# A retention stage run whole, and run as 16 pieces between other products, in a two-block network on one core

## The chip, the cores and the metric

The kernel runs on one core of one Trainium2 chip. The metric is the device time of one execution in microseconds (us), and lower is better. Five engines work beside each other: TensorE (PE, with its weight loads shown as PEld), VectorE (DVE), ScalarE (ACT), GpSimd (POOL) and SyncE (SP), which issues the kernel's DMAs from one queue in order. Each engine takes its instructions in the order in which the program puts them on it, and waits on semaphores for the others.

## The reference, cut to what matters

The network has two blocks of two layers each. The change touches the second block alone, and in it one part of each layer: from the normed input `h` (1024 tokens, 1024 features) one product gives the inputs of three branches, whose results are joined by `w_out`.

```python
za, xb, q, k, v, g = jnp.split(proj, splits, axis=-1)
ya = spatial_gating(jax.nn.gelu(za), a_vnorm_g[l], a_ws[l], a_bs[l])   # gated mixing over tokens
yb = multiscale_pool(xb, b_w[l], b_scale[l])                            # pooling
yc = retention(q, k, v, g, c_norm_g[l])                                 # retention
```

Retention has 8 heads of 64 features. In the reference it goes by chunks of tokens, in order, with a state per head that is carried on:

```python
scores = jnp.einsum('bnthd,bnshd->bnhts', qc, kc) * d_intra
y_intra = jnp.einsum('bnhts,bnshe->bnthe', scores, vc)
kv = jnp.einsum('bnshd,bnshe->nbhde', kc * k_dec[:, :, None], vc)
def step(state, kv_n):
    return state * chunk_dec[None, :, None, None] + kv_n, state
y_cross = jnp.einsum('bnthd,nbhde->bnthe', qc * q_dec[:, :, None], s_prev)
```

Mean and variance per head are then taken out, and the result is multiplied by `silu(g)`.

## The kernel before, in words

Large products (called dense here) keep float32 accuracy with two parts to each operand, `hi` and `lo`, and three matrix products per block (`mm3`, L221 to L223), each with 128 rows, 128 weight columns and 512 moving columns. A dense result of 128 x 512 takes 8 blocks, so 24 matmul instructions, and collects in one PSUM bank. `gemm_tm` makes results with tokens on partitions, the first two tokens' tiles as a pair; `gemm_fm` makes results with features on partitions. Weights come by DMA (`wraw`, three buffers) and are split by `load_w`: ACT casts `whi` (L205), DVE or, one time in six, POOL subtracts `wlo` (L192, L190). Four pairs of buffers hold weights (`wt`). After each dense result both call `tick`, which takes one step of a generator in `self.side`, if there is one; the first block uses this for its convolution.

`layer2` (per layer, twice) runs in this order:

1. `rotate`: queries and keys, rotated on DVE and written to DRAM by head (`rq_d`, `rk_d`).
2. `gemm_tm("v", ...)`: 8 tiles of values, each copied by ACT into `V` (L1073).
3. `retention`: 8 tiles of 128 tokens, one after the other.
4. `pooling_in`: four dense results, the inputs `xb` of the pooling.
5. `spatial_in`: 8 dense results `za` (L1094), the inputs of the gated mixing.
6. `pooling`: POOL adds shifted copies (L1157 to L1161), DVE finishes (L1164 to L1166).
7. `retention_out`: the retention result is scaled on DVE (L1296, L1297), the gate's 8 dense results follow, with `pooling_out` and `spatial` between them.

In one tile of `retention` TensorE has these small float32 products, each of which the trace shows as two instructions, except the transposes:

- scores, L1238: 8 products `sc<-rq,rk` of 64 rows, 128 columns. Even heads lie on partitions 0 to 63 (g = 0), odd heads on 64 to 127 (g = 1); first all four of one half, then all four of the other. DVE multiplies by the decay mask into `ra` (L1240).
- transposes of the keys, L1245: 4, `sc<-ident,rk`, which DVE scales into `kd` (L1247). Not for the last tile.
- intra-tile outputs, L1252: 8 products `ax<-rv,ra` of 128 rows, 64 columns, into `pi`.
- cross outputs, L1260: 8 products `sc<-rst,rq` of 64 rows with the state `rst`, again half by half; DVE scales (L1261) and adds (L1262). Not for the first tile.
- the tile's share of the state, L1270: 8 products `ax<-rv,kd` into `pv`; POOL and DVE make the next state (L1276, L1277). Not for the last tile.

Then the means: DVE reduces (L1280), POOL scales and subtracts into `V` (L1281, L1283), ACT squares (L1285), DVE reduces (L1286), and POOL raises to the power -0.5 (L179).

PSUM has three pools: `mm` (3 banks, dense results), `ax` (2 banks, `pi` and `pv` among others) and `sc` (3 banks, scores, transposes, cross outputs). A scheduler orders the instructions of each engine by the order of the code and by when buffers come free; in the built program it puts a few dense products of stage 4 between the tiles of retention.

```python
            self.gemm_tm("v", I["w_tm_v"][l], 512, toks(), ev_v)
            with left(f"re{l}", 2) as rp, left(f"re1{l}", 1) as r1:
                self.retention(l, V, rp, r1)
```

## Time and profile before

| | us |
|---|---|
| three timed runs, median | 3703.01 |
| lowest and highest of them | 3697.34, 3711.04 |
| span of the profiled execution | 3717.3 |
| TensorE busy in it | 3510.1 (94%) |
| VectorE, ScalarE, GpSimd busy | 2445.2, 1242.8, 849.8 |

The profiled execution is another one than the three timed runs; of its own time only the span is given, from its first instruction to its last, and what lies around it is not in the table. Its stages can be found by their lines. In the first layer of the second block the retention's first TensorE instruction starts 1565.3 us into the span and its last ends at 1627.4; in the second layer they are at 2684.2 and 2785.65.

### The profile page before, as it was taken

What the parts mean: (1) busy time and instruction counts of PE and PEld (TensorE: products, weight loads), DVE (VectorE), ACT (ScalarE), POOL (GpSimd) and SP (SyncE); (2) the same over time, 40 slices, a digit from 0 to 9 for tenths busy, and PEclk for the clock granted to TensorE, in tenths of its full rate; (3) what the DMA queues carried; (4) which work ended last, traced back from release to release, by engine and by line L of the source; (5) the groups of instructions that cost most, each with busy time, mean ns of one, the idle gap of its engine ahead of it and who ended that gap; (6) DMA issues with size and microseconds to landing.
All of it is one profiled execution on the core that took longest, in us unless ns stands there. A gap on an engine that the chain in (4) does not pass through costs nothing.

```text
span 3717.3 us, 46878 instructions
## 1 busy us (share of the span) xinstructions
PE 3510.1 (94%) x17414; PEld 2809.0 (76%) x17414; DVE 2445.2 (66%) x3786; ACT 1242.8 (33%) x2249; POOL 849.8 (23%) x700
## 2 busy tenths in 40 slices
PE   7979889999897999999999998999999989999998
PEld 4868656677875678887878777887897778888787
DVE  5965368568553866364599998437244479999645
ACT  4114146341241752113343333223102333443322
POOL 4332232112313222040132321001022032322100
PEclk9999989999997999999999999999959999999999
DMA  6222155542213243314322223424311622221532
GB/s 197 75 75 69 55 167 172 181 125 75 77 61 102 75 129 134 102 36 143 120 83 80 81 77 109 140 85 153 94 32 60 188 72 82 80 80 63 176 99 92
DMA packets 242965, 380.69 MB, mean 102 GB/s; under 512 B 24048, under 2 KB 99760, under 8 KB 242224
## 3 DMA queue, kind: packets, MB, share of 16 engines
q1 hardware_dynamic: 242736, 377.69, 31.9%
q8 instruction: 137, 2.24, 0.3%
q14 instruction: 92, 0.75, 0.1%
HBM read 280.35 MB, written 97.26 MB: 102 GB/s over the span
## 4 chain that ended last, share of the span: by engine, by line
PE 66%; DVE 14%; DMA 8%; issue 5%; ACT 2%; POOL 2%; SPq 1%; DVEq 0%; POOLq 0%; ACTq 0%
PE mm L221 11%; PE mm L222 11%; PE mm L223 11%; PE ax L221 3%; PE ax L223 3%; PE ax L222 3%; PE sc L221 3%; PE sc L222 3%; PE sc L223 3%; DVE wlo L192 2%; PE mm L943 2%; DVE ca L494 2%; PE mm L929 2%; DMA wraw<-ks_d 2%; DVE cv L1431 1%
## 5 line engine op out<-in xcount | busy, mean ns | idle before, releaser
L221 PE MATMUL mm<-hi,whi 128*128 128x512 f32 (+1 forms) x1780 | 693.7, 390 | 21.5 <-ACT whi L205 9.9
L223 PE MATMUL mm<-hi,wlo 128*128 128x512 f32 (+1 forms) x1780 | 690.3, 388 | 4.8 <-DVE wlo L192 3.7
L222 PE MATMUL mm<-lo,whi 128*128 128x512 f32 (+1 forms) x1780 | 691.4, 388 | 1.2 <-DVE lo L1616 1.1
L205 ACT CAST whi<-wraw 128x512 fp32r<-128x512 f32 (+3 forms) x412 | 232.1, 583 | 539.3 <-PE mm L222 258.7
L221 PEld LDWEIGHTS mm<-hi,whi 128*128 128x128 f32 x1780 | 339.0, 190 | 96.2 <-ACT whi L205 10.3
L223 PEld LDWEIGHTS mm<-hi,wlo 128*128 128x128 f32 x1780 | 338.6, 190 | 76.9 <-DVE wlo L192 6.0
L222 PEld LDWEIGHTS mm<-lo,whi 128*128 128x128 f32 x1780 | 339.2, 191 | 72.2 <-DVE lo L1616 3.1
L192 DVE TENSOR_TENSOR wlo<-wraw,whi 128x512 fp32r<-128x512 f32 (+2 forms) x320 | 228.7, 727 | 245.8 <-ACT whi L205 244.8
L221 PE MATMUL sc<-hi,whi 128*128 128x512 f32 x732 | 290.2, 397 | 13.1 <-ACT y L1496 7.5
L190 POOL TENSOR_TENSOR wlo<-wraw,whi 128x512 fp32r<-128x512 f32 (+3 forms) x92 | 132.7, 1449 | 723.6 <-ACT whi L205 645.3
L222 PE MATMUL sc<-lo,whi 128*128 128x512 f32 x732 | 290.1, 396 | 2.1 <-DVE lo L1616 2.1
L223 PE MATMUL sc<-hi,wlo 128*128 128x512 f32 x732 | 290.1, 396 | 1.2 <-DVE wlo L192 1.1
L221 PE MATMUL mm<-whi,hi 128*128 128x512 f32 (+2 forms) x704 | 260.7, 370 | 30.7 <-DVE ggt L341 16.4
L222 PE MATMUL mm<-wlo,hi 128*128 128x512 f32 (+2 forms) x704 | 256.9, 365 | 3.4 <-POOL wlo L190 2.3
L223 PE MATMUL mm<-whi,lo 128*128 128x512 f32 (+2 forms) x704 | 257.2, 365 | 0.0
L494 DVE SCALAR_TENSOR_TENSOR ca<-u,wh,ca 128x1024 f32<-128x1024 f32 (+1 forms) x180 | 197.6, 1142 | 0.6
L223 PE MATMUL ax<-hi,wlo 128*128 128x512 f32 x456 | 180.2, 395 | 2.4 <-DVE wlo L192 2.4
L221 PE MATMUL ax<-hi,whi 128*128 128x512 f32 x456 | 179.9, 395 | 1.9 <-DVE xn L1347 1.4
L222 PE MATMUL ax<-lo,whi 128*128 128x512 f32 x456 | 179.6, 394 | 0.0
L192 DVE TENSOR_TENSOR wlo<-wr,whi 128x512 fp32r<-128x512 f32 x200 | 175.8, 890 | 0.0
L221 PEld LDWEIGHTS sc<-hi,whi 128*128 128x128 f32 x732 | 139.4, 190 | 45.8 <-ACT y L1496 7.9
L221 PEld LDWEIGHTS mm<-whi,hi 128*128 128x128 f32 x704 | 135.0, 192 | 50.8 <-issue 19.1
(378 smaller groups left out, 6864.3 us busy)
## 6 DMA issues: line engine op xcount, KB each, us to landing
wr<-in_w_up SPq DMA_DIRECT2D x80, 512.0 KB
wraw<-in_w_fm SPq DMA_DIRECT2D x108, 256.0 KB
wm<-in_w_mod SPq DMA_DIRECT2D x96, 256.0 KB
wraw<-in_w_down SPq DMA_DIRECT2D x96, 256.0 KB
hid_d<-fth SPq DMA_DIRECT2D x44, 512.0 KB
wraw<-hid_d SPq DMA_DIRECT2D x88, 256.0 KB
wraw<-in_w_out SPq DMA_DIRECT2D x80, 256.0 KB
yl<-y_d SPq DMA_DIRECT2D x64, 256.0 KB
```

The source lines that it names most:

```text
L190: nc.gpsimd.tensor_sub(out, x, f(hi))
L192: nc.vector.tensor_sub(out, x, f(hi))
L205: nc.scalar.copy(hi[:, c], r)
L221: nc.tensor.matmul(ps, sh, mh, start=start, stop=False)
L222: nc.tensor.matmul(ps, sh, ml, start=False, stop=False)
L223: nc.tensor.matmul(ps, sl, mh, start=False, stop=stop)
L494: nc.vector.scalar_tensor_tensor(a, u[:, j:j + n], wh[:, c, j:j + 1], a, op0=ALU.mult, op1=ALU.add)
L929: nc.tensor.transpose(pt[:, j * 128:j * 128 + 128], P[:, h, kt * 128:kt * 128 + 128], self.ident)
L943: nc.tensor.matmul(po[half[u], :256], vst[:, vt, 64 * v:64 * v + 64], PT[kt][:, u * 256:u * 256 + 256], start=kt == 0, stop=kt == nkt - 1)
L1431: nc.vector.scalar_tensor_tensor(t[:, o:], x[:, 0:S - o], wc(2 - o), t[:, o:], op0=ALU.mult, op1=ALU.add)
```

## The change

`retention` becomes a generator with two `yield`s per tile, so 16 steps. It starts before the values' products and is stepped by `tick`. `RT = 2` lets the first two ticks pass; then one step follows each dense result of `gemm_tm("v")`, of `pooling_in` and of `spatial_in`. The first step of a tile (a-piece) holds the scores, the transposes and the loads of the next tile's queries and keys; the second (b-piece) holds the cross outputs, the state's products and the intra-tile outputs, in this order. In scores and cross outputs the two halves of the rows now take turns, each into its own PSUM bank, with TensorE's order fixed by `in_order`. `pooling` moves ahead of `spatial_in`. The rest of the diff takes comments out, so line numbers after the change are 1 to 21 higher.

```diff
+RT = 2
...
-            self.gemm_tm("v", I["w_tm_v"][l], 512, toks(), ev_v)
             with left(f"re{l}", 2) as rp, left(f"re1{l}", 1) as r1:
-                self.retention(l, V, rp, r1)
+
+                self.ticks = [None] * RT
+                self.side = self.retention(l, V, rp, r1)
+                self.gemm_tm("v", I["w_tm_v"][l], 512, toks(), ev_v)
                 with self.right(f"mp{l}") as mp, self.right(f"sg{l}") as sp:
                     xb = self.pooling_in(l, W, lat, mp)
+                    self.pooling(l, xb, mp)
                     z = self.spatial_in(l, toks, sp)
-                    self.pooling(l, xb, mp)
+                    run(self.side)
+                    self.side = None
...
+        halves = [(g, slice(64 * g, 64 * g + 64)) for g in range(2)]
+        nxt = load(0)
+        for j in range(8):
+            q, k = nxt
+
+            ps = [self.psC.tile([128, 512], F32, name="sc", tag="sc") for g in range(2)]
+            with self.in_order():
+                for m in range(4):
+                    for g, r in halves:
+                        nc.tensor.matmul(ps[g][:, m * 128:m * 128 + 128], k[r, m, :], q[r, m, :], start=True, stop=True)
...
+                nxt = load(j + 1)
+            yield
...
             if j:
+                pc = [self.psC.tile([128, 4, 64], F32, name="sc", tag="sc") for g in range(2)]
+                with self.in_order():
+                    for m in range(4):
+                        for g, r in halves:
+                            nc.tensor.matmul(pc[g][:, m, :], q[r, m, :], st[r, m, :], start=True, stop=True)
...
+            pi = self.psB.tile([128, 512], F32, name="ax", tag="ax")
+            for h in range(8):
+                hv = slice(h * 64, h * 64 + 64)
+                nc.tensor.matmul(pi[:, hv], A[h % 2][:, h // 2, :], V[:, j, hv], start=True, stop=True)
...
             self.rsqrt(ss[:, j, :], ss[:, j, :], 1.0 / 64)
+            yield
```

TensorE, first layer, with buffer numbers, which tell apart the PSUM banks of the two halves. Before, the end of one tile and the start of the next: the scores of one half, then those of the other.

```order
L1260 MATMUL sc_14394<-rst_14341,rq_14353 128x64 x4
L1270 MATMUL ax_14401<-rv_13303,kd_14376 64x64 x8
L1238 MATMUL sc_14426<-rq_14422,rk_14423 128x128 x4
L1238 MATMUL sc_14433<-rq_14422,rk_14423 128x128 x4
L1245 MATMUL sc_14440<-ident_78,rk_14423 128x128 x4
L221 MATMUL mm_14697<-hi_13154,whi_14687 128x512
```

After, the start of an a-piece: the last dense product of a pooling input, then scores that go to the two banks in turn (the pattern goes on for eight products).

```order
L223 MATMUL mm_14390<-lo_13179,whi_14380 128x512
L224 MATMUL mm_14390<-hi_13178,wlo_14381 128x512
L1250 MATMUL sc_14416<-rq_14295,rk_14296 128x128
L1250 MATMUL sc_14417<-rq_14295,rk_14296 128x128
L1250 MATMUL sc_14416<-rq_14295,rk_14296 128x128
```

TensorE took four products of one half before it turned to the other; now each product's neighbour is of the other half, and a whole dense result stands before the piece.

TensorE, first layer, without numbers. Before, one tile of retention, with the four dense products (L221 to L223) that the scheduler put into it:

```order
L1270 MATMUL ax<-rv,kd 64x64 x8
L1238 MATMUL sc<-rq,rk 128x128 x8
L1245 MATMUL sc<-ident,rk 128x128 x4
L223 MATMUL mm<-hi,wlo 128x512
L221 MATMUL mm<-hi,whi 128x512
L222 MATMUL mm<-lo,whi 128x512
L223 MATMUL mm<-hi,wlo 128x512
L1252 MATMUL ax<-rv,ra 128x64
L1260 MATMUL sc<-rst,rq 128x64 x4
L1252 MATMUL ax<-rv,ra 128x64 x7
```

After, the one place where two pieces of a tile (the sixth) stand close to each other, because the pair at the start of `spatial_in` ticks twice:

```order
L1250 MATMUL sc<-rq,rk 128x128 x8
L1259 MATMUL sc<-ident,rk 128x128 x4
L222 MATMUL mm<-whi,hi 128x512
L1271 MATMUL sc<-rst,rq 128x64
L223 MATMUL mm<-wlo,hi 128x512
L224 MATMUL mm<-whi,lo 128x512
L222 MATMUL mm<-whi,hi 128x512
L1271 MATMUL sc<-rst,rq 128x64 x7
L1280 MATMUL ax<-rv,kd 64x64 x8
L1284 MATMUL ax<-rv,ra 128x64 x8
```

Here four dense products stand between the pieces as before; at the other places 24 do.

POOL, first layer. Before, the last tiles' means, then the pooling's large adds (L1157 to L1161) in a row:

```order
L1281 TENSOR_SCALAR rmu<-rmu 128x8
L1283 TENSOR_TENSOR rv<-ry,rmu 128x512
L179 TENSOR_TENSOR rss<-rss,mhalf 128x8
L1157 TENSOR_TENSOR s_15081<-xb_14685 128x1024
L190 TENSOR_TENSOR wlo<-wraw,whi 128x512
L1158 TENSOR_TENSOR s_15082<-s_15081 128x1024
```

After, the same adds (L1162 to L1166) with the state's and the means' steps of two tiles behind and between them:

```order
L1162 TENSOR_TENSOR s_14658<-xb_14378 128x1024
L191 TENSOR_TENSOR wlo<-wraw,whi 128x512
L1163 TENSOR_TENSOR s_14659<-s_14658 128x1024
L1291 TENSOR_TENSOR rst<-rst,rgam 128x256
L1301 TENSOR_SCALAR rmu<-rmu 128x8
L1159 MEMSET s_14670 128x16
L1303 TENSOR_TENSOR rv<-ry,rmu 128x512
L1159 MEMSET s_14671 128x16
L180 TENSOR_TENSOR rss<-rss,mhalf 128x8
L1162 TENSOR_TENSOR s_14670<-xb_14517 128x1024
```

The pooling moved from behind the retention into its tiles 3 to 5. On every engine the rest of the program keeps its order; the counts of instructions are the same.

## Rows read from the trace of the kernel before

**Rows 1.** The page: span, TensorE's busy time, its granted clock in 40 slices.

```profile
span 3717.3 us, 46878 instructions
...
PEclk9999989999997999999999999999959999999999
```

**Rows 2.** Windows: length, busy time by engine, granted clock, DMA share, GB/s; by stage.

```profile
1565.30:1627.40 62.10, 61.93 (x533) 56.79 (x532) 39.75 (x77) 8.66 (x15) 23.58 (x27) 0.89 0.26 78
1627.40:1701.50 74.10, 73.02 (x315) 58.79 (x315) 35.03 (x48) 20.13 (x43) 24.27 (x15) 1.00 0.14 43
...
2684.20:2785.65 101.45, 99.93 (x533) 91.61 (x533) 42.13 (x80) 9.33 (x16) 26.05 (x28) 0.53 0.16 48
```

**Rows 3.** Windows again, at the falls of the granted clock.

```profile
1580.65:1584.35 3.70, 3.70 (x31) 3.56 (x30) 1.60 (x4) 0.63 (x1) 1.83 (x2) 1.00 0.27 75
1584.35:1591.17 6.82, 6.82 (x43) 6.02 (x42) 5.21 (x9) 0.63 (x1) 1.91 (x4) 0.50 0.16 48
...
1594.59:1601.41 6.82, 6.82 (x44) 6.26 (x44) 4.45 (x8) 0.63 (x1) 2.05 (x4) 0.50 0.13 38
...
2684.17:2690.27 6.10, 4.58 (x38) 4.03 (x38) 3.62 (x6) 2.15 (x5) 1.40 (x1) 1.00 0.46 139
2690.27:2789.25 98.98, 98.98 (x506) 90.44 (x506) 41.83 (x81) 7.17 (x12) 25.92 (x29) 0.50 0.14 41
```

**Rows 4.** Timeline of TensorE, one tile at full clock: start, length, line, tiles, count.

```profile
1602.19 1.10 PE L1260 MATMUL sc<-rst,rq 64*128 64x64 f32 x8
1603.22 1.77 PE L1252 MATMUL ax<-rv,ra 128*128 128x64 f32 x14
1604.93 1.10 PE L1260 MATMUL sc<-rst,rq 64*128 64x64 f32 x8
1605.96 0.69 PE L1270 MATMUL ax<-rv,kd 128*64 128x64 f32 x16
1606.58 1.71 PE L1238 MATMUL sc<-rq,rk 64*128 64x128 f32 x16
1608.22 0.66 PE L1245 MATMUL sc<-ident,rk 128*128 128x128 f32 x4
1608.63 0.48 PE L222 MATMUL mm<-lo,whi 128*128 128x512 f32 x1
1608.94 0.39 PE L223 MATMUL mm<-hi,wlo 128*128 128x512 f32 x1
```

**Rows 5.** Timeline of TensorE, the scores at half clock, second layer.

```profile
2732.15 3.09 PE L1238 MATMUL sc<-rq,rk 64*128 64x128 f32 x16
```

**Rows 6.** Timeline of TensorE where L1238 and L1260 take turns by chance.

```profile
1623.21 0.27 PE L1238 MATMUL sc<-rq,rk 64*128 64x128 f32 x1
1623.26 0.27 PE L1260 MATMUL sc<-rst,rq 64*128 64x64 f32 x1
1623.32 0.27 PE L1238 MATMUL sc<-rq,rk 64*128 64x128 f32 x1
```

**Rows 7.** Timeline of ACT: copies of two values' tiles, one dense result apart.

```profile
1537.38 0.59 ACT L1073 COPY rv<-mm 128x512 f32<-128x512 f32 x1 [5.01 <-PE mm L223]
1542.98 0.59 ACT L1073 COPY rv<-mm 128x512 f32<-128x512 f32 x1 [5.01 <-PE mm L223]
```

**Rows 8.** Timeline of DVE, POOL and ACT in one tile; in brackets idle time and its releaser.

```profile
1607.94 0.68 DVE L1280 TENSOR_REDUCE rmu<-ry 128x8 f32<-128x512 f32 x1
...
1608.54 1.28 DVE L1240 TENSOR_TENSOR ra<-sc,dm 128x512 f32<-128x512 f32 x2
...
1609.73 0.68 DVE L1247 TENSOR_TENSOR kd<-sc,rdec 128x512 f32<-128x512 f32 x1
...
1610.82 0.69 DVE L1286 TENSOR_REDUCE rss<-rsq 128x8 f32<-128x512 f32 x1 [0.41 <-ACT rsq L1285]
```

**Rows 9.** Timeline during the pooling's POOL adds: two DVE subtractions, TensorE's wait.

```profile
1650.26 5.16 DVE L192 TENSOR_TENSOR wlo<-wraw,whi 128x512 fp32r<-128x512 f32 x2
...
1655.48 0.50 PE L222 MATMUL mm<-wlo,hi 128*128 128x512 f32 x1 [1.08 <-DVE wlo L192]
```

More of the change, by code (lines that the diff above doesn't have):

```diff
@@ L1225, in retention, with load @@
         st = None
-        for j in range(8):
+        def load(j):
             tk = slice(j * 128, j * 128 + 128)
@@ L1232, in retention @@
                     out=t, in_=d[:, :, :, tk].rearrange("(m h) a f t -> (h a f) m t", h=2))
+            return q, k
+        halves = [(g, slice(64 * g, 64 * g + 64)) for g in range(2)]
[7 more added lines that the diff above has]
+                        nc.tensor.matmul(ps[g][:, m * 128:m * 128 + 128], k[r, m, :], q[r, m, :], start=True, stop=True)
             A = []
             for g in range(2):
-                ps = self.psC.tile([128, 512], F32, name="sc", tag="sc")
-                r = slice(64 * g, 64 * g + 64)
-                for m in range(4):
-                    nc.tensor.matmul(ps[:, m * 128:m * 128 + 128], k[r, m, :], q[r, m, :], start=True, stop=True)
                 a = rp.tile([128, 4, 128], F32, name="ra", bufs=3)
-                nc.vector.tensor_mul(a, ps.rearrange("p (h t) -> p h t", h=4), dm[:, g::2, :])
+                nc.vector.tensor_mul(a, ps[g].rearrange("p (h t) -> p h t", h=4), dm[:, g::2, :])
                 A.append(a)
@@ L1248, in retention @@
                                         dec[:, 0, :].unsqueeze(2).broadcast_to([128, 8, 64]), op=ALU.mult)
-            pi = self.psB.tile([128, 512], F32, name="ax", tag="ax")
-            for h in range(8):
-                hv = slice(h * 64, h * 64 + 64)
-                nc.tensor.matmul(pi[:, hv], A[h % 2][:, h // 2, :], V[:, j, hv], start=True, stop=True)
+                nxt = load(j + 1)
+            yield
             y = rp.tile([128, 8, 64], F32, name="ry", tag="ry", bufs=3)
-            piv = pi.rearrange("p (h d) -> p h d", h=8)
             if j:
-                for g in range(2):
-                    pc = self.psC.tile([128, 4, 64], F32, name="sc", tag="sc")
-                    r = slice(64 * g, 64 * g + 64)
-                    for m in range(4):
-                        nc.tensor.matmul(pc[:, m, :], q[r, m, :], st[r, m, :], start=True, stop=True)
-                    nc.vector.tensor_tensor(y[:, g::2, :], pc, dec[:, 1, g::2].unsqueeze(2).broadcast_to([128, 4, 64]), op=ALU.mult)
-                nc.vector.tensor_add(y, y, piv)
-            else:
-                nc.scalar.copy(y, piv)
+                pc = [self.psC.tile([128, 4, 64], F32, name="sc", tag="sc") for g in range(2)]
[3 more added lines that the diff above has]
+                            nc.tensor.matmul(pc[g][:, m, :], q[r, m, :], st[r, m, :], start=True, stop=True)
+                for g in range(2):
+                    nc.vector.tensor_tensor(y[:, g::2, :], pc[g], dec[:, 1, g::2].unsqueeze(2).broadcast_to([128, 4, 64]),
+                                            op=ALU.mult)
             if j < 7:
@@ L1270, in retention @@
                     nc.tensor.matmul(pv[r, (h // 2) * 64:(h // 2) * 64 + 64], kd[:, h, :], V[:, j, hv], start=True, stop=True)
+            pi = self.psB.tile([128, 512], F32, name="ax", tag="ax")
+            for h in range(8):
+                hv = slice(h * 64, h * 64 + 64)
+                nc.tensor.matmul(pi[:, hv], A[h % 2][:, h // 2, :], V[:, j, hv], start=True, stop=True)
+            if j < 7:
                 ns = rp.tile([128, 4, 64], F32, name="rst")
@@ L1278, in retention @@
                 st = ns
+            piv = pi.rearrange("p (h d) -> p h d", h=8)
+            if j:
+                nc.vector.tensor_add(y, y, piv)
+            else:
+                nc.scalar.copy(y, piv)
             mu = rp.tile([128, 8], F32, name="rmu")
```

## The prediction

> **What bounds the kernel now.** I read the page first. TensorE is busy in 94% of a span of 3717.3 us, so a time can only fall where TensorE has less to do or does it faster. The page's line of the granted clock has a 5 in the 30th of 40 slices, which is 2695 to 2788 us, and 7 to 9 elsewhere [rows 1]: there TensorE runs at the lower of its two levels, 1.2 for 2.4 GHz. Next I took the windows of the retention in both layers [rows 2]. The same 533 instructions take 62.10 us at a mean clock of 0.89 in the first layer and 101.45 us at 0.53 in the second. TensorE is busy in 61.93 and 99.93 us of them; DVE has 40 to 42 us of work in each, POOL 24 to 26. So TensorE itself is the limit, and its small products and their clock are the price, not a chain of waits.
>
> Then the clock's falls [rows 3]. In the second layer it falls at 2690.27, behind a stretch in which TensorE waited 1.5 of 6.1 us, and stays down for 98.98 us, in all of which TensorE is busy. In the first layer it falls twice for 6.82 us; ahead of the first fall lie 3.7 us with only cross outputs (L1260) and intra-tile outputs (L1252), 31 instructions, without any wait. Busy time alone does not hold the clock up; these small products do not.
>
> Last, one tile at full clock, by the starts of its groups [rows 4]. The scores (L1238) take 1608.22 - 1606.58 = 1.64 us, 103 ns for each of 16; transposes 0.41; the state's products (L1270) 0.62; cross outputs 1.03 per half, 2.06; intra-tile outputs 1.71 for 14, 1.95 for 16. Together 6.68 us. Eight tiles, the first without cross outputs (4.62), the last without transposes and state's products (5.65), make 50.3 us. At half clock the 16 scores last 3.09 us for 1.71 [rows 5].
>
> **The change part by part.** A dense result takes 1542.98 - 1537.38 = 5.60 us, or 0.233 us for each of its 24 products [rows 7]. In program order 23 dense products lie among the retention's rows in the first layer and 24 in the second. Their time leaves 62.1 - 5.4 = 56.7 us and 101.45 - 5.6 = 95.9 us for the retention, 152.6 us in both. Dense work is neither added nor removed, so only these 152.6 us change.
>
> *The halves in turn.* The trace of before has one place where products of the two halves mix: L1238 of one tile's second half and L1260 of the next work's first half start alternately, and a pair takes 1623.32 - 1623.21 = 0.11 us [rows 6]. Apart, the two take 0.103 + 0.129 = 0.23 us [rows 4]. I take 0.11 for each pair of scores and of cross outputs: 8 pairs, 0.89 us, for 1.64 and 2.06. The bounds are half of what they take now (0.82) and no gain at all (1.64 and 2.06); the mixed rows are the same lines and the same sizes, so I stand by them. A full tile is then 0.89 + 0.41 + 0.89 + 1.95 + 0.62 = 4.76 us, the first 3.87, the last 3.73, and a layer 36.2 us.
>
> *The clock.* A b-piece is the longest small stretch, 0.89 + 0.62 + 1.95 = 3.5 us, and a dense result of 5.6 us stands on either side but at one place. The clock fell behind 3.7 us of L1260 and L1252 alone; in a b-piece L1252 has 1.95 us, and the faster products stand ahead of it. Over the first 19 us of the first layer's retention, with L1270, L1238 and four dense products in each tile, it stayed up. I take full clock throughout.
>
> Weighed against this: the Trainium skill (TensorE: Matmul & The Clock Gate, section HAM oscillation) says that the clock drops where the engine goes idle between bursts. By that rule nothing in the pieces could lower it. The rows differ, 98.98 us at 0.50 without idle time [rows 3], and the measurement decides.
>
> *Edges.* The first dense product behind small ones starts 0.31 us ahead of the next, for 0.233 [rows 4]: 0.08 us for each of 16 pieces, 1.3 us a layer. So 37.5 us a layer, 75.0 in both, and 152.6 - 75.0 = 77.6 us saved.
>
> *Waits in the pieces.* A b-piece needs `ra` and `kd` from DVE: 1.28 + 0.68 = 2.0 us behind the a-piece [rows 8], hidden by 5.6 us of dense work. What may stand ahead of them on DVE is the tile before: its step L1286 waits for POOL's and ACT's, and ends 1611.51 - 1607.94 = 3.6 us behind the start of L1280 [rows 8], then come two scalings of `V`. That is some 6 us behind a b-piece, and the next a-piece ends 5.6 + 1.3 us behind it: the cover is there, with 3 to 4 us to spare before the b-piece. In the sixth tile only four dense products (0.93 us) and the cross outputs lie between; there TensorE may wait up to 1 us. During the pooling's large POOL adds DVE slows down: two subtractions of 0.7 us each took 5.16, and TensorE waited 1.08 for them [rows 9]. These adds now fall into tiles 3 to 5 of the retention, and `rst`, `rmu` and the subtraction queue behind them on POOL; DVE waits for POOL in turn, and the next `ra` stands behind that wait. I allow 2 us a layer for all of this, 0 to 8 as bounds. The wait at the first tile of the second layer (1.5 us [rows 3]) goes, since 24 dense products now cover it; it is in the 95.9.
>
> *Queues.* SP's loads of queries and keys stand between weight loads, as before; those for the third to fifth tile now precede the last part of the pooling's weights and the first of `za`. They wait for pieces 20 to 30 us ahead of the weights' use, so I cost them at nothing; without that cover each late weight would cost a few us. The first weights of the pooling lose the retention as cover; their buffer comes free early in the last values' result, which leaves 4 us and a b-piece for two casts and two subtractions.
>
> **Sum.** 77.6 - 4 = 73.6 us off the span of 3717.3 gives 3643.7. That span is 14.3 us above the median of the timed runs, 3703.0, and the runs differ by 13.7 among themselves. Why is not shown; if it is the length of the half-clock stretch, the median run has less to gain. So I take 71 us off the median: **3632 us**.
>
> **The rivals.**
>
> 1. *The halves do not overlap.* Then scores stay at 1.64 and cross outputs at 2.06: 8 x 0.75 + 7 x 1.17 = 14.2 us a layer, 28 in both, 3660. For it: rows 6 are one place, where the products were of different kinds. Against it: same sizes, same halves.
> 2. *Each edge drains TensorE.* With 16 pieces there are 32 edges a layer between dense and small products; at the whole 0.39 us of a dense product for each, 12.5 us a layer, 25 in both, 3657. Against it: the dense product behind the transposes came 0.08 us late [rows 4]. The Trainium skill (TensorEngine Tiling (Array Packing), section Key Properties) says that a change of tiling mode drains the engine, which speaks for this rival. By it the split would pay at every edge.
> 3. *Waits take the gain.* If DVE were late at each of the 8 b-pieces of a layer by 4.5 us, 72 us would go, and the time would be 3704, no change. It needs DVE to fall some 8 us behind in each tile. Against it: DVE has 40 + 35 us of work [rows 2] in a stretch that will be about 121 us a layer.
> 4. *The clock falls in the pieces.* A fall in the first layer lasted 6.82 us [rows 3], in which half, 3.4, is lost. One at each of the 32 pieces of both layers costs 109 us: 3741, slower. From 21 falls on it eats the gain. For it: 99 us at half clock with four dense products in each tile did not bring the clock back [rows 3]. Against it: now 24 do stand there, for four.
>
> That the pieces are not where they should be is excluded by the program's order.
>
> **How the numbers follow.** Forecast 0.79, between 3618 and 3648; no overlap 0.07; drains 0.03; waits 0.04; clock 0.05; something else 0.02. The range goes from 3612, which is 77.6 us and the other runs' spread below the median, to 3662, behind the first two rivals and the bound of 16 us of waits in both layers. About 0.5%, 18.5 us, is what a measurement can tell from no change. Faster by more: the forecast, the first two rivals and part of the rest, 0.90. Within 0.5%: 0.04. Slower: 0.06.
>
> **What would show it.** The line of the clock should have no 5 in its middle, and windows over the spread retention should read 1.00 or close. Scores and cross outputs should have starts 50 to 60 ns apart. From the end of the third values' tile to the last piece there should be 15 dense results, 84 us, and 37.5 us of pieces. TensorE's waits inside the pieces should add up to under 5 us a layer, the longest at the sixth tile. The prediction is wrong if a DVE or POOL step ends long waits ahead of L1280 or L1284, or if the windows around the b-pieces show 0.50.

## The result and the profile after

The changed kernel takes 3657.66 us, median of four runs (3651.94 to 3664.98), the kernel before 3705.76 (3697.34 to 3711.04), 48 us less. The ratio is 0.9882, 95% interval 0.9834 to 0.993; ratios here are estimates from the fast runs of a set (within 1.5% of the fastest) and differ a little from the quotient of the medians (0.987 here). The direction is the predicted one; the size is not. The forecast was 3632, 71 us less, with a chance of 0.79 for 3618 to 3648; the measured time lies outside of that, and inside the wider range of 3612 to 3662. Between the two profiled executions the gain is larger, 3717.3 - 3655.3 = 62.0 us of span. The time is the span and 1.8 us around it (3657.07 for 3655.3), so the profiled execution of the changed kernel lies amid its runs, and that of the kernel before, 3719, above all four of its own. That gap of 14 us turns out to be about half of the miss of 26.

The page of the changed kernel answers [rows 1]: the 5 in the 30th slice of the clock's line is gone.

```profile
span 3655.3 us, 46869 instructions
...
PEclk9989989999898999999999999999999999999999
```

Windows answer [rows 2, 3] (length, busy time of PE, PEld, DVE, ACT and POOL, granted clock, DMA share, GB/s): from the first to the last piece in each layer, then two parts of the second layer.

```profile
1536.76:1663.56 126.80, 125.00 (x868) 102.45 (x869) 62.80 (x106) 25.53 (x50) 42.64 (x37) 1.00 0.17 51
2643.15:2775.31 132.16, 129.22 (x868) 106.25 (x869) 62.15 (x106) 23.79 (x48) 41.35 (x37) 0.96 0.16 49
2731.41:2736.40 4.99, 2.05 (x15) 1.26 (x13) 3.18 (x5) 0.08 (x1) 1.31 (x1) 1.00 0.18 53
2736.40:2746.64 10.24, 10.24 (x57) 9.04 (x53) 3.25 (x6) 0.63 (x1) 1.85 (x3) 0.50 0.09 27
```

Of the 868 TensorE instructions 508 are the retention's own; the other 360 are the 15 dense results that the forecast counted, 84.0 us at 5.60. So the retention now costs 126.8 - 84.0 = 42.8 us in the first layer and 48.2 in the second, 91.0 together, for 152.6 before. 61.6 us less: that is the difference of the spans but for 0.4 us. The forecast had 79.0, its 4 us of waits included.

TensorE's timeline for one tile answers [rows 4 to 6] (start, length, line, count; dense rows left out).

```profile
1552.23 1.16 PE L1250 MATMUL sc<-rq,rk 64*128 64x128 f32 x16
1553.32 0.66 PE L1259 MATMUL sc<-ident,rk 128*128 128x128 f32 x4
...
1559.51 1.11 PE L1271 MATMUL sc<-rst,rq 64*128 64x64 f32 x16
1560.55 0.69 PE L1280 MATMUL ax<-rv,kd 128*64 128x64 f32 x16
1561.16 2.00 PE L1284 MATMUL ax<-rv,ra 128*128 128x64 f32 x16
```

By the starts, the scores take 1.09 us for 1.64 before and the cross outputs 1.04 for 2.06. Two products in turn cost 0.13 to 0.14 us, where the forecast took 0.11.

Last, the sixth tile of the second layer, where only four dense products lie between the two pieces: the timeline of all engines, with idle time and its releaser in brackets.

```profile
2721.67 1.89 POOL L1165 TENSOR_TENSOR s<-s 128x1024 f32<-128x1024 f32 x1
...
2725.00 2.38 POOL L1166 TENSOR_TENSOR s<-s 128x1024 f32<-128x1024 f32 x1
2727.34 1.04 POOL L1303 TENSOR_TENSOR rv<-ry,rmu 128x512 f32<-128x512 f32 x1
...
2728.42 0.63 ACT L1305 ACTIVATE rsq<-rv 128x512 f32<-128x512 f32 x1 [11.84 <-POOL rv L1303]
...
2729.83 0.69 DVE L1306 TENSOR_REDUCE rss<-rsq 128x8 f32<-128x512 f32 x1
...
2731.08 1.65 POOL L180 TENSOR_TENSOR rss<-rss,mhalf 128x8 f32<-128x8 f32 x1 [2.69 <-DVE rss L175]
...
2732.76 0.69 DVE L1317 TENSOR_TENSOR rv<-rv,rss 128x512 f32<-128x512 f32 x1 [1.76 <-POOL rss L180]
...
2734.09 1.28 DVE L1254 TENSOR_TENSOR ra<-sc,dm 128x512 f32<-128x512 f32 x2
2734.83 0.43 PE L1271 MATMUL sc<-rst,rq 64*128 64x64 f32 x2 [2.94 <-DVE ra L1254]
```

It is read from the bottom. TensorE stands 2.94 us for `ra`. DVE is late with `ra` since the scaling of the tile before (L1317) stands ahead of it and waits 1.76 us for POOL's power (L180). That power is late since the tile's subtraction (L1303) had queued behind the pooling's adds (L1165, L1166). 1.6 us behind the wait's end the clock falls for the 10.24 us of the fourth window above.

In the first layer the same chain stands at the same place, and the wait is shorter; no fall follows it (1.00 in the first window above).

```profile
1627.77 0.43 PE L1271 MATMUL sc<-rst,rq 64*128 64x64 f32 x2 [1.64 <-DVE ra L1254]
```

### The profile page after: what moved, and what is told of

It reads as the page before. It is cut to its first block, busy times and chain, and to the rows that moved or that the text cites. A ratio compares the mean times of both kernels' runs of the same rounds, so it can differ in the third digit from the quotient of the medians.

```text
span 3655.3 us, 46869 instructions
## 1 busy us (share of the span) xinstructions
PE 3441.3 (94%) x17414; PEld 2743.3 (75%) x17414; DVE 2447.5 (67%) x3786; ACT 1239.3 (34%) x2249; POOL 850.9 (23%) x700
## 4 chain that ended last, share of the span: by engine, by line
PE 61%; DVE 14%; DMA 9%; issue 6%; ACT 3%; POOL 3%; SPq 1%; DVEq 0%; POOLq 0%; ACTq 0%
PE mm L222 11%; PE mm L223 11%; PE mm L224 11%; PE ax L223 3%; PE ax L224 3%; PE ax L222 3%; PE sc L223 3%; PE sc L222 3%; PE sc L224 3%; DVE wlo L193 2%; DMA wraw<-ks_d 2%; DVE cv L1452 2%; PE mm L944 2%; PE mm L930 2%; DMA qs_d<-qlo 1%
## 5 line engine op out<-in xcount | busy, mean ns | idle before, releaser
L223 PE MATMUL mm<-lo,whi 128*128 128x512 f32 (+1 forms) x1780 | 688.1, 387 | 1.2 <-DVE lo L1637 1.1
L223 PEld LDWEIGHTS mm<-lo,whi 128*128 128x128 f32 x1780 | 337.3, 189 | 72.2 <-DVE lo L1637 3.1
L193 DVE TENSOR_TENSOR wlo<-wraw,whi 128x512 fp32r<-128x512 f32 (+2 forms) x320 | 226.2, 720 | 120.0 <-ACT whi L206 118.9
L223 PE MATMUL sc<-lo,whi 128*128 128x512 f32 x732 | 289.6, 396 | 2.2 <-DVE lo L1637 2.1
L223 PE MATMUL mm<-wlo,hi 128*128 128x512 f32 (+2 forms) x704 | 259.7, 369 | 2.2 <-POOL wlo L191 2.2
L223 PE MATMUL ax<-lo,whi 128*128 128x512 f32 x456 | 179.4, 393 | 0.0
L193 DVE TENSOR_TENSOR wlo<-wr,whi 128x512 fp32r<-128x512 f32 x200 | 174.2, 882 | 0.0
```

What stands on the lines that cost most here:

```text
L193: nc.vector.tensor_sub(out, x, f(hi))
L223: nc.tensor.matmul(ps, sh, ml, start=False, stop=False)
```

## The experiments

Theory at the start: a gain of two parts, small products that overlap and a clock that stays up, less a wait at the sixth tile; and a baseline execution that held the clock low for longer than most. The rivals are in each expectation. In each set all kernels and the kernel before ran on one chip. The changed kernel was timed in a set of its own and in that of the late scaling and of the single turns. Its 3657.66 us beside the split alone, the turns alone and one tick is thus a comparison across sets; the one-tick kernel, timed on two chips, took 3647.15 and 3649.17 us.

### The kernel before, again

> The kernel before, unchanged, profiled in another execution. The forecast started from one profiled execution with a span of 3717.3 us, above all four timed runs (3697 to 3711), and 62.0 us lie between the two profiled spans where the timed runs differ by 48. Theory: that execution held TensorE's clock low for longer than most; then another one has a span some 5 to 20 us shorter, a half-clock stretch in the second layer's retention clearly shorter than 98.98 us (or fewer falls elsewhere), and the same TensorE work at the same price per product. Rival: the stretch is 99 us here as well, and the difference is waits or transfers; then the mean clock of the runs does not follow their spans. The mean granted clock of each run tells: if the clock is the cause, 0.001 of it should go with about 3.7 us.

Measured: 3676.55 to 3723.78 us in ten runs, the unchanged kernel beside it 3681.85 to 3731.67 in seventeen. The granted clock goes with it, from 0.971 at the fastest run (3676.55) to 0.954 at the slowest (3731.67): 55 us for 0.017, or 3.2 us for 0.001. The profiled execution has a span of 3679.5 us, 37.8 shorter, where 5 to 20 were expected. Its windows: the half-clock stretch in the second layer, then the whole second layer's retention, 65.50 us for the 101.45 of [rows 2].

```profile
2689.20:2706.30 17.10, 17.10 (x103) 15.74 (x101) 7.83 (x15) 2.10 (x4) 5.15 (x7) 0.50 0.28 88
2683.50:2749.00 65.50, 64.91 (x534) 59.62 (x534) 41.89 (x80) 9.29 (x16) 24.93 (x28) 0.87 0.25 74
```

So the 99 us of [rows 3] are no fixed price of the code. The forecast had taken one draw for it.

### The split alone, with the halves in blocks

```diff
-                for m in range(4):
-                    for g, r in halves:
+                for g, r in halves:
+                    for m in range(4):
```

The same edit is made for the cross outputs.

> The changed kernel, but the scores and the cross outputs take first the four products of one half of the rows, then the four of the other, as before the change; the split into 16 pieces stays. Theory: taking turns is what makes the halves overlap. Then the scores go back from 1.09 to about 1.64 us and the cross outputs from 1.04 to about 2.06: 8 x 0.55 + 7 x 1.02 = 11.5 us a layer, 23 us in both, a time of about 3681 at an unchanged clock. Rival A: the longer b-pieces (2.06 + 0.62 + 1.81 = 4.5 us) also bring the clock down; with a fall of 6.8 us at half clock at each of 14 of them the time goes to about 3728. Rival B: with dense work on both sides the halves overlap in blocks as well, and the time stays at 3658.

Measured: 3675.76 us (3663.98 to 3680.3), 0.9886 of before, and one fall of 6.8 us in each layer, both behind a wait at the sixth tile (0.94 and 2.11 us). TensorE's timeline:

```profile
1563.65 1.60 PE L1271 MATMUL sc<-rst,rq 64*128 64x64 f32 x16
...
1573.38 1.71 PE L1250 MATMUL sc<-rq,rk 64*128 64x128 f32 x16
```

By the starts, scores are back at 1.64 us, cross outputs only at 1.53: 0.55 x 8 + 0.49 x 7 = 7.8 us a layer, 15.7 in both, where 23 were expected. The time is 18 us above the changed kernel's 3657.66 of the other set; the ratios beside each one's own kernel before, 0.9886 and 0.9882, do not tell the two apart. The turns do make the halves overlap, by the trace; what they add in time on top of the split is some 16 to 18 us. Rival A falls: b-pieces of 4.0 us did not bring the clock down between dense results, but for the two falls behind waits.

### The turns alone, retention whole

The scores and the cross outputs take turns as in the changed kernel; everything else is as before.

> The kernel before with one part of the change alone: scores and cross outputs take the halves of the rows in turn, but retention still runs whole, between the values and the pooling inputs. Theory: the clock falls because small products stand close together, whatever their order; then the second layer's long half-clock stretch stays, and the gain is 11.5 us in the first layer and up to 23 at half clock in the second: about 3675, 10 to 35 us below before. Rival A: the blocks of one half are what lets the clock fall; then it stays at 1.00 and the time comes within 10 us of the changed kernel's 3658. Rival B: shorter products leave DVE (40 us a layer) as the limit, waits take the gain, and the time stays within 5 us of before.

Measured: 3670.05 us (3667.34 to 3673.11), 0.9876. Windows over the retention of both layers:

```profile
1568.48:1625.54 57.06, 55.33 (x557) 47.21 (x556) 44.19 (x83) 10.33 (x18) 23.91 (x27) 1.00 0.28 85
2679.64:2741.40 61.76, 58.36 (x557) 50.06 (x556) 44.28 (x83) 10.27 (x18) 23.87 (x27) 0.94 0.26 79
```

The clock stays up but for one fall of 6.8 us, though retention is not split. So my reason for the clock, that dense results on either side keep it up, is not the only one: each half of the change does it nearly alone. The waits for DVE's `ra` are longer (57.06 - 55.33 = 1.7 us, and 3.4): in the second layer 2.3 us of them are the wait at the first tile, for 0.59 to 1.71 in the kernel before. The fall starts 0.9 us behind that wait and lasts 6.8 us, where it lasted 17 to 99 with the halves in blocks. The time lies 12 us above the changed kernel's 3657.66 of the other set.

### Which turns

Two kernels, each the kernel before with one product's halves in turn.

> The kernel before; only the scores take the halves in turn, the cross outputs stay in blocks. Both halves in turn alone brought the second layer's half-clock time from 99 or 17 us down to 10. Theory: products of 64 rows in blocks of one half are what pulls the clock down, and the scores, 1.64 of 3.7 us of such blocks in a tile, are less than half of it; then the clock is in between: half-clock time in both layers' retention of 10 to 45 us, mean clock of the runs 0.963 to 0.972, time 3675 to 3700. Rival A: the scores decide it; half-clock time at most 15 us, 3676. Rival B: only the cross outputs decide it; the runs spread as those of before, 3677 to 3732, less 9 us.

> The kernel before; only the cross outputs take the halves in turn, the scores stay in blocks. Theory (blocks of one half pull the clock down, whichever product they belong to): half-clock time in between, 10 to 45 us, mean clock of the runs 0.963 to 0.972, time 3670 to 3700. Rival A (the scores decide): the runs spread as those of before, 3677 to 3732, less 14 us. Rival B (the cross outputs decide): half-clock time at most 15 us and about 3674.

Measured: scores in turn 3683.97 us (3673.14 to 3698.87), 0.9959, beside 3704.99; cross outputs in turn 3693.5 (3659.64 to 3708.07), 0.9975, interval up to 1.0019. Windows over the stretch with falls, second layer: scores in turn, a mean of 0.71 over 71.7 us, so some 41 us at half clock in five falls, the longest of 17;

```profile
2683.40:2755.10 71.70, 71.28 (x513) 63.53 (x513) 41.51 (x81) 6.47 (x11) 25.80 (x29) 0.71 0.17 51
```

cross outputs in turn, one fall of 92.2 us.

```profile
2682.30:2774.50 92.20, 92.20 (x509) 83.27 (x509) 41.85 (x81) 6.86 (x12) 24.49 (x29) 0.50 0.14 43
```

Neither is enough alone. That the scores do more is not shown: the runs with cross outputs in turn cover those with scores in turn at both ends. With the 6.8 us of the first layer the scores in turn have some 48 us at half clock, just above the 10 to 45 expected, and a time within the 3675 to 3700; the 92.2 us with cross outputs in turn lie far above, and their runs spread over 48 us, nearly as widely as those of before.

The two layers differ. In the first, where no wait stands ahead of the falls of the kernel before, there was no fall in the one execution with cross outputs in turn, nor in the one with both in turn; with scores in turn it was 6.8 us, and 13.6 to 27.3 in seven executions with both in blocks.

### The changed kernel, again

> The changed kernel, unchanged, timed beside the kernel before and the other three of this set. Theory: its TensorE stretch with pieces has only one fall of the clock, behind the wait at the sixth tile of the second layer, so its time repeats: within 8 us of 3658, where the kernel before spreads over more than 40 us with its clock. Rival: it spreads as widely as the kernel before (3652 to 3700), and its four runs so far were lucky.

Measured: 3662.89 us in nine runs (3652.31 to 3674.05), 0.9885, interval 0.9856 to 0.9915. Its spread, 22 us, is wider than I expected but under half of that of the kernel before beside it (3668.56 to 3723.30). The wait of 2.94 us came back at the same place. The fall, here 13.7 us, starts 1.1 us before that wait ends, so that the products behind the wait cannot have begun it.

### One tick at the pair

```diff
-                self.tick()
+                if name != "za" or p is ps[-1]: self.tick()
```

> The changed kernel, but the pair at the start of the gated mixing's inputs ticks once, so that two dense results, not four products, stand between the two pieces of the sixth tile; its later pieces come one dense result later each. Theory: the waits of 1.64 and 2.94 us at that place and the 10.24 us at half clock behind the second one come from the short distance; without them the two layers lose some 5 and 8 us less, minus nothing, and the time falls by about 10 us, to 3648, with a clock of 1.00 over both layers' pieces. Rival: POOL's pooling adds delay DVE so far that the next pieces wait instead; then the waits move to another tile and the time stays within 3 us of 3658.

> The changed kernel with one tick at the pair, as in an earlier run (3647.2 us, 0.9817 of before), beside the other kernels of this set on one chip. Theory: it holds 10 us below the changed kernel, 0.981 to 0.985 of before, with the same two waits and the fall gone. Rival: the 10 us were the chip's; then it comes at 0.988 of before.

Measured: 3647.15 us (3642.57 to 3658.84), 0.9817, interval 0.978 to 0.9855; on another chip 3649.17 (3647.69 to 3655.69), 0.9857, interval 0.9813 to 0.99. The second ratio lies just outside the 0.981 to 0.985 expected, and its interval holds the rival's 0.988 too; the times, 8 to 16 us below the changed kernel's two medians in other sets, and the windows speak for the theory. Windows of the second one over both layers' pieces:

```profile
1541.15:1671.30 130.15, 129.98 (x893) 106.68 (x893) 62.82 (x106) 26.72 (x53) 42.79 (x37) 1.00 0.16 50
2643.53:2773.05 129.52, 129.52 (x892) 106.36 (x893) 61.84 (x106) 24.80 (x51) 41.16 (x37) 1.00 0.16 50
```

TensorE stands still for 0.17 us in the first and not at all in the second, and the clock reads 1.00. With 16 dense results (89.6 us, and one dense product of 0.23 at the start of the first window) the retention costs 40.3 and 39.9 us: 80.2, for the forecast's 79.0. The 10 us were the sixth tile's. The first one's profiled execution has the same windows, 130.35 and 129.72 us at 1.00, and yet a span of 3657.1 us for 3646.0. The mean clock over the span is 0.970 for 0.973, and 0.003 of 3650 us are 11: falls in other stages move a single span by as much as this remedy.

### The scaling taken out of the pieces

```diff
-            nc.vector.tensor_tensor(y3, y3, ss[:, j, :].unsqueeze(2).broadcast_to([128, 8, 64]), op=ALU.mult)
-            nc.vector.tensor_mul(y, y, ng)
...
+            nc.vector.tensor_tensor(g3, g3, ss[:, j, :].unsqueeze(2).broadcast_to([128, 8, 64]), op=ALU.mult)
+            nc.vector.tensor_mul(g, g, ng)
```

> The changed kernel, but the retention's scaling by its inverse deviation and by the norm's weights is applied to the gated result, not to the values, so that these 16 DVE steps a layer leave the pieces; the two pieces of the sixth tile still stand four products apart. Theory: the waits of 1.64 and 2.94 us there come from ra's step on DVE behind a scaling that waits for POOL's power; without it TensorE waits 0.3 to 0.9 us there, the fall of 10.24 us behind it goes, and the time is about 3649. Rival: ra is late because DVE and POOL slow each other down during the pooling; then the waits stay over 1.5 us and the time at 3658. A loss is possible in the gate's stage, where the 16 steps now lie, if DVE is late there.

> The changed kernel with both remedies at once: one tick at the pair of the gated mixing's inputs, and the scaling by the inverse deviation applied to the gated result. Theory: either remedy alone takes away both waits and the fall, so both together gain nothing over one: 3645 to 3657, no wait over 1 us in the pieces, no fall of the clock in them. Rival: the scaling's steps still cost in the pieces where it stays (the cross outputs of the fifth tile wait 0.6 us in each layer) and cost nothing in the gate's stage; then it is 1 to 3 us below one tick alone.

Measured: with the scaling late alone 3657.3 us (3653.08 to 3662.06), 0.9882, which is no difference that shows against the changed kernel's 0.9885 on the same chip; with both remedies 3658.99 (3651.39 to 3660.84), 0.9876, 10 us above one tick alone on the same chip. Yet in the first of them both waits of the sixth tile and the fall are gone. One wait of TensorE is left around the second layer's pieces, by releaser (total, times, longest); it is for the first keys' DMA and stands in the changed kernel as well:

```profile
PE sc L1250 <- DMA rk<-rk_d: 0.8, 1, 0.8
```

So the cause of the wait is what the timeline says, DVE's scaling behind POOL's power; but the remedy gives the gain back later. Windows from the last piece to about the gate's last transposes, one tick alone:

```profile
1671.30:1737.00 65.70, 64.04 (x282) 47.97 (x282) 35.86 (x55) 23.57 (x42) 8.39 (x7) 1.00 0.46 147
2773.00:2839.50 66.50, 64.02 (x283) 48.05 (x283) 35.72 (x56) 23.87 (x43) 7.32 (x6) 1.00 0.46 145
```

and with both remedies:

```profile
1670.90:1739.40 68.50, 66.14 (x289) 49.58 (x288) 45.64 (x71) 24.63 (x44) 8.75 (x7) 0.99 0.48 148
2776.30:2847.00 70.70, 66.92 (x289) 49.47 (x289) 46.94 (x71) 24.28 (x44) 8.65 (x7) 0.98 0.47 145
```

DVE has 10 to 11 us more there, and the stretch is 2.8 and 4.2 us longer. Some 1.5 us of each are the 6 or 7 more instructions that TensorE has in the window, at 0.233 us each. It stands still for 0.7 and 1.3 us more: the output projection's operands (`ylo`, L193) now queue behind the scaling. And at the end of each stretch the clock falls, for 3.4 and 6.8 us from 1737.7 and 2843.6 on, where it does not with one tick alone; the kernel with the scaling late has these two falls too. Half of the 10.2 us and the 2.0 us of waits are 7 of the 10 us; where the rest lies was not found. The 0.6 us that the expectation puts at the fifth tile stand in the first layer alone (cross outputs 1.63 us for 1.04).

### Nine stretches for sixteen pieces

With one tick at the pair, the `yield` at a tile's end is left out but for the last tile.

> The changed kernel with one tick at the pair, and without the break at a tile's end: the second piece of a tile and the first of the next follow each other, so that a layer has 9 stretches of small products, of up to 5.0 us, for 16. Theory: a dense result takes 0.09 to 0.17 us more between small products than among dense ones, so seven edges fewer a layer save about 1 us each layer and the time is 1 to 3 us below one tick alone, if the clock stays up. Rival A: stretches of 5.0 us without dense products bring the clock down, 6.8 us at half clock at each of some 14 of them, 48 us: about 3695. Rival B: DVE, with a whole tile's steps between two stretches, is late by 1 us or more at each; then 10 to 20 us more than one tick alone.

Measured: 3648.69 us (3644.37 to 3657.9), 0.9855, the same as one tick beside it. No fall in the pieces of either layer: 5.0 us of small products, part of them in turn, do not lower the clock here. TensorE's waits in the first layer, by releaser (total, times, longest):

```profile
PE mm L223 <- DVE wlo L193: 3.4, 2, 2.3
```

So what the fewer edges may save can be lost again to late weights' parts; how much the edges save was not told apart.

### Where the long fall of the kernel before starts

In [rows 3] the fall at 2690.27 comes 2 us behind a wait. One edit takes that wait away: the first tile's scores and transposes stand one dense result earlier, ahead of the last values' tile.

```diff
-            self.gemm_tm("v", I["w_tm_v"][l], 512, toks(), ev_v)
             with left(f"re{l}", 2) as rp, left(f"re1{l}", 1) as r1:
-                self.retention(l, V, rp, r1)
+                ret = self.retention(l, V, rp, r1)
+                self.gemm_tm("v", I["w_tm_v"][l], 512, toks(), ev_v, {6: lambda: next(ret)}); run(ret)
...
+            if j == 0: yield
```

> The kernel before, whole retention and halves in blocks; only the first tile's scores and transposes stand one dense result earlier, ahead of the last values' tile, so that DVE's mask and decay steps lie beside it. In the kernel before TensorE waits 0.6 to 1.5 us for them at the start of the second layer's retention, and a fall of the clock starts 2 us behind that wait, of 17.1 or 99.0 us. Theory: that wait starts the long fall. Without it the second layer looks like the first, with 7 to 28 us at half clock in both layers together instead of 44 to 113, the runs spread less, and their median is 3665 to 3685. Rival: the blocks of 64-row products bring the clock down by themselves, whenever they are run; then the second layer still has falls of 17 us or more, and the runs keep the spread of before, 3668 to 3731, median some 2 us below it.

Measured: 3676.52 us (3671.68 to 3694.76, ten runs) beside 3714.47, a ratio of 0.9918, interval 0.9883 to 0.9952. The windows over the second layer's retention, from the first tile's intra-tile outputs on, in two executions (the second is the repetition below):

```profile
2688.90:2744.90 56.00, 56.00 (x522) 51.44 (x521) 40.66 (x78) 9.12 (x16) 24.94 (x28) 1.00 0.29 86
```

```profile
2686.00:2741.90 55.90, 55.90 (x521) 51.38 (x520) 40.48 (x77) 9.19 (x16) 24.95 (x28) 1.00 0.29 86
```

The same small products, in the same blocks of one half, with 4 dense ones to a tile, run at 1.00 here. Four more profiled executions then looked at the wait and the stretch together.

> The kernel before, unchanged, profiled once more. Two executions: TensorE's wait at the second layer's first intra-tile product 1.52 us, stretch 99.0, span 3717.3; wait 0.59, stretch 17.1, span 3679.5. Theory: the span is about 3659 us plus half of the time at half clock in both layers' retention (3661.0 and 3657.3 so far), and a wait over 1 us goes with a stretch of over 60 us, one under 1 us with less than 30. Rival: the stretch has any length whatever the wait was.

> The kernel before, unchanged, profiled once more; the same expectations: span 3659 us plus half of the half-clock time of both layers' retention, within 4 us; wait over 1 us with a stretch over 60 us, under 1 us with less than 30. Rival: any length whatever the wait.

> The kernel before, unchanged, profiled once more; the same expectations: span 3659 us plus half of the half-clock time of both layers' retention, within 4 us; wait over 1 us with a stretch over 60 us, under 1 us with less than 30. Rival: any length whatever the wait.

> The kernel before with the first tile's scores and transposes one dense result early, profiled once more. Theory (the wait starts the long stretch): no wait over 0.5 us at the first tile and no fall over 30 us in the second layer's retention, span 3665 to 3685. Rival: a second-layer stretch of 30 us or more appears here too, and the earlier execution was lucky.

| execution | TensorE's wait, us | second layer at half clock, us | both layers at half clock, us | span, us |
|---|---|---|---|---|
| [rows 3] | 1.52 | 99.0 | 112.6 | 3717.3 |
| again | 0.59 | 17.1 | 44.4 | 3679.5 |
| third | 1.71 | 99.0 | 119.5 | 3725.7 |
| fourth | 1.49 | 99.0 | 119.5 | 3724.7 |
| fifth | 0.59 | 75.1 | 95.6 | 3710.7 |
| first tile early | none | none | 23.9 | 3674.9 |
| first tile early, again | none | none | 13.6 | 3676.5 |

The wait in TensorE's timeline, third execution, then fifth, with the fifth's stretch:

```profile
2695.98 0.43 PE L1252 MATMUL ax<-rv,ra 128*128 128x64 f32 x2 [1.71 <-DVE ra L1240]
```

```profile
2690.04 0.66 PE L1252 MATMUL ax<-rv,ra 128*128 128x64 f32 x4 [0.59 <-DVE ra L1240]
```

```profile
2690.70:2765.80 75.10, 75.10 (x397) 68.94 (x396) 31.52 (x60) 4.62 (x8) 19.23 (x23) 0.50 0.17 51
```

In all five a fall starts 0.7 to 2.6 us behind the start of the product that had waited, and in the second layer, where nothing waited, there was none. How long it lasts does not follow the wait as I had expected: 0.59 us went with 17.1 and with 75.1. The span less half of the half-clock time is 3657 to 3666 in the five, so one quantity carries most of the spread of the kernel before; two of the five lie more than the expected 4 us from 3659, and the repetition with the first tile early comes to 3669.7. The edit also moves 20 small instructions out of the stretch; a wait put in by itself was not tried, so that the wait alone is the trigger is supported, not shown. Nor does a wait always bring a fall: the 1.64 us in the changed kernel's first layer had none.

Put beside each other, the runs show a pattern, from one to five executions each, that no run was made to test. Behind a wait of 0.59 to 1.71 us the clock stayed down for 17 to 99 us where scores ran in blocks of one half, with four dense products to a tile. It stayed down for 3.4 to 13.7 us behind or within waits of 0.94 to 2.94 us, where scores took turns or whole dense results stood between the pieces. By this either half of the change shortens the fall, and the first tile's early products keep it from starting.

## Why the prediction was right and wrong

**Right: what bounds it, and where the gain comes from.** The retention's own share of TensorE's time went from 152.6 to 91.0 us, and the rest of the span is the same within 0.4 us. The dense results between the pieces are 15, as counted; the clock's line has lost its 5.

**Right in kind, 3 us too small: the products.** A full tile takes 1.09 + 0.41 + 1.04 + 0.62 + 1.81 = 4.97 us for 4.76, a layer 37.7 for 36.2. The pair at 0.11 us [rows 6] was a pair of unlike products at the seam of two groups; in a row of eight pairs it is 0.13 to 0.14. For the cross outputs the forecast's 0.89 lay below half of their 2.06, a bound that it worked out for the scores alone; they came to 1.04. The intra-tile outputs, at 1.81 for 1.95, gave a part back.

**Edges: too small by a half.** A dense result between pieces takes 5.68 to 5.80 us for 5.60, 0.08 to 0.20 for the 0.08 of the forecast: 2.1 us a layer for 1.3. The rival in which each edge drains TensorE needed 0.39 at each of two edges; it did not come. By the Trainium skill (TensorEngine Tiling (Array Packing), section Key Properties) a change of tiling mode drains the engine; if that is in these 0.08 to 0.20 us, it is small here; no run takes it by itself.

**Waits: the place was right, the price was not.** The forecast put the longest wait at the sixth tile, and named the step of DVE that would stand ahead of `ra`. It gave it up to 1 us; it took 1.64 and 2.94, and the second brought a fall of 10.24 us, of which 5.1 are lost. The step that failed is "3 to 4 us to spare": it was worked out for a tile without the pooling's adds, and the allowance for these adds was made as a sum for the layer, not at the tile where four dense products are all the cover. The three terms together, pieces 3, edges 1.6 and waits with the fall 7.4 beyond the 4 allowed, are the 12.0 us by which 91.0 exceeds 79.0. The 11.4 us of waits and fall are, by the starts, 2.4 and 8.4 us at the sixth tile and 0.6 at the fifth of the first layer. One tick fewer takes 10.8 of them away (80.2).

**Queues: put at nothing.** The first scores now wait for the DMA of their keys, 0.17 us in the first layer and 0.84 in the second; no weights came late in the pieces.

**Wrong: the step from the profiled execution to the median.** The forecast saw that the profiled span lay 14 us above the median and that the length of the half-clock stretch might be why, and then took 71 of the 73.6 us off the median all the same. It was why, for the most part: the mean clock follows the runs, and five executions of the kernel before have 44 to 120 us at half clock in the retention, two with spans below that of [rows 1] and two above. So the step that failed here is the 71 us: a gain read from one long execution was taken off the median. Taking the 14 us off the gain gives 59.3 and 3644; with the 12.0 above, 3656, for 3657.66 measured.

**The clock: right in its result, incomplete in its reason.** That the small products do not hold the clock up, as the forecast says of them, is no rule: in blocks, with four dense products to a tile, they ran 56.0 us at 1.00 once TensorE's wait ahead of them was gone. The forecast had that wait among its rows and costed it at 1.5 us; the fall behind it costs up to 49.5. The Trainium skill (TensorE: Matmul & The Clock Gate, section HAM oscillation) lays the clock's falls to idle time between bursts. I had set the 98.98 us at 0.50 without idle time against it. The runs agree with it in so far as idle time stands ahead of the fall of the second layer. How 0.59 to 1.71 us of waiting lead to 17 to 99 us without any, they do not tell, and the first layer's falls of 6.8 to 17.1 us have no such wait ahead. That the full clock held in fifteen of the sixteen tiles' pieces is what was forecast; that turns or distance would each have done most of it was not in the forecast's reason.

**The rivals.** "Halves do not overlap" and "drains" are out by the rows above. "Waits take the gain" came at one tile for eight. "The clock falls in the pieces" came once, behind a wait, for the 21 falls that it needed. The third part of the change, the pooling ahead of `spatial_in`, was not taken back in any run; its adds stand ahead of the sixth tile's wait, and what the move does by itself is open.

So of the gain some 11 us, or 15 with one tick, are work saved: without what the half-clock time in the retention costs (half of 112.6 us before, of 10.2 after) the spans are 3661.0 and 3650.2, and 3646.0 with one tick. Single spans differ by as much elsewhere; the retention's own windows, less what their mean clock lost, give 98.1, 85.9 and 80.2 us, so 12 and 18. The rest is the clock, and much of that could be had without this change, by the first tile's scores alone (3676.52) or by the turns alone (3670.05). The best kernels here are the changed one with one tick at the pair, 3647 to 3649, and the one with nine stretches, 3648.69.

## What to carry to other kernels

A price read in one execution at the lower clock is one draw: before a gain is taken from it, look whether the runs spread by more than the gain's error, and whether their granted clock goes with their time. Look for the short wait ahead of a long half-clock stretch; to remove that wait may be worth much of what a rewrite of the stretch brings (on one chip 3676.52 us, and 3649.17 with the rewrite and one tick, for 3714.47 before). Where pieces are interleaved with other work, the cover is set at the place where two pieces stand closest, and it is to be costed there, with every queue that feeds it.

## What the runs showed of the hardware

- TensorE can stay at 0.50 for 75 to 99 us while it is busy without a gap, and most of the same instructions run at 1.00 in another execution (17.1 us at 0.50), or all of them with the first tile's products one dense result early (56.0 us at 1.00).
- 64-row float32 products whose halves take turns cost 0.13 to 0.14 us a pair, for 0.19 to 0.26 in blocks of one half (1.53 us for cross outputs in one group, 2.06 in two groups of four, 1.64 for scores).
- POOL's power on 128 x 8 elements took 1.65 us (L180 in the stretch above), longer than its subtraction of 128 x 512 at 1.04 (L1303), beside the pooling's adds of 1.89 to 2.38 us for 128 x 1024 (L1165, L1166). The power's 1.65 us held in all 16 tiles; the scaling of 128 x 8 (L1301) took 0.20 us at the median and 1.27 at most.
